# The opening of a hybrid RG-LRU / attention block: norm chain split between two engines, transposes placed ahead of the scale columns, shift sums kept in the query rows' tile

## Chip, cores and metric

One core of one Trainium2 chip runs the whole block. The metric is the device time of one execution in microseconds. Engines are named as in the profile: PE (TensorE), with its weight loads as PEld, DVE (VectorE), ACT (ScalarE), POOL (GpSimd) and SP (SyncE, which issues most DMAs).

## The reference

One layer (DEPTH = 1) over a sequence of 2048 rows of width 1024, batch 1, all in fp32:

```python
mod = silu(c) @ w_ada + b_ada
shift, scale, gate = split(mod, 3)
h = layer_norm(x) * (1 + scale) + shift
xr, zr, q, k, v, za, fl = split(h @ w_in)            # 512 columns each, fl: 8
xc = causal_depthwise_conv(xr, conv_w, conv_b)       # 4 taps
y_r = rms_norm(rg_lru(xc)) * silu(zr)
y_a = rms_norm(forgetting_attention(q, k, v, log_sigmoid(fl + b_fgate))) * silu(za)
y = concat([y_r, y_a]) @ w_out
out = layer_norm(2 ** 0.25 * x + gate * y) * ln_gain + ln_bias
```

What matters here is the beginning: `shift` and `scale` are products of one row, silu(c), with 1024 x 1024 parts of `w_ada`; `h` needs them both and the normalised x; the first projection is xr, from the first 512 columns of `w_in`.

## The kernel before

The sequence is cut into four chunks (ci = 0 to 3) of 512 rows, each chunk into four tiles of 128 rows, and the width of 1024 into eight slices k of 128. The work is written as one long Python program. Buffers are tiles of named tags with a fixed number of slots (t2: 10 slots of 2 KB a partition, r4: 8 of 4 KB, xr: 5, H: 8; PSUM banks: A 3, O 1, B 2, C 2). A tile waits until the one that had its slot before is done. A planner lays out each engine's order from simulated times, the earlier line of the program first among what is ready. `tc.issue_after(ins)` forces what follows to stand behind `ins` in the queue of the engine that `ins` is on. On the chip each engine then takes its queue strictly in that order. `tick()` moves the first of the small waiting chains (generators in `chains`) by one `yield`; `flush()` drains them.

The opening, up to about 145 us, goes through these stages:

1. **Warm-up and norm of chunk 0.** `spin(n)` issues n matmuls on zeros. `load_x(0)` loads four tiles as two halves each; `norm_x` calls `norm_tile` (L270) for each: `ln_stats` (L241) takes the statistics on DVE (L244, L246), adds epsilon (`ve`, L248), POOL raises to the power -0.5 (`rs`, L250), and DVE multiplies minus the mean by that (`nm`, L252). Then ACT (L274) or POOL (L276) applies scale and bias to each half.
2. **Chunk 0 in fp32 (loop at L759).** For each k: `scale_col(k)` (L638) loads a 128-column block of `w_ada` as `wadab`, sums part of it on DVE (L646, L648) for k of 2 and more, and does the rest as narrow matmuls `psc`; the result is one column of `Acol`, 1 + scale (L653). `load_w32(k)` loads a slice of `w_in` and splits it into a high and a low part (ACT L661, POOL L663). `make_h32(0, k, xs)` (L380) transposes four tiles on PE (`ptr`, L387), and ACT (L388) and DVE (L389) write h times scale as a high and a low part; POOL joins them for later (L378). `xr32` (L610) does twelve matmuls `pj` of slice k - 1. `col_max` (L167, tile `xam`) takes the largest magnitude of the weights, whose scale `xmax_fin` (L793) finishes with two small PE steps `pam`. From k = 5 on, the tiles of chunk 1 are normalised. At k = 7 the slabs 0 to 4 of the shift are begun by `shift_slab` (L746): each loads two tiles `wsh` in t2; ACT multiplies by the column of silu(c) (L231), POOL adds (L234) into `pa`, which is the tile of slab 0.
3. **Chunk 1 in fp32 (loop at L801).** Again `make_h32` and `xr32`, two k behind. The slabs 5 to 7 of the shift go to DVE: slab 5 is multiplied in place (L225) and becomes `va`, the others are added to it (L227). At k = 3 chunk 2 is loaded into t2, eight halves, and `va` and `pa` are added (L812). At k = 4 sixteen narrow matmuls `pada` make the shift column `Bcol`, and `make_scale` (L337) is put in `chains`; it finds the common scale `sh` through `all_max` (L148), with PE steps `pam`, and scales `Ash`, `Bcol` and `B16`. At k = 3 to 6 the weights are split to fp16 (`split_T`, L316, L317), and at k = 4 to 7 chunk 2 is normalised.
4. **Chunks 2 and 3 in fp16 (loops at L852 and L868).** `make_hk` (L394) transposes (L398), ACT writes h (`hf`, L400), ACT and DVE split it to fp16 (`hT`, L354, L355); `xr_k` projects slice k - 1; `finish_h` turns the kept h of chunks 0 and 1 into the same form.

After this come v, the gates, k, z, q and attention, which the diff does not touch. `QB`, four tiles of 67 rows for the query side of attention, is allocated at L905; the first use of its other rows is a memset on POOL (L1302), of which the planner puts the first four at the very beginning (2.9 us).

Of the kernel before, what the change touches and what calls it, by code (L numbers as in the profile page):

```python
# [10 lines left out]
F16 = mybir.dt.float16  # L11
F32 = mybir.dt.float32
# [26 lines left out]
def hybrid_mixer(  # L39
# [200 lines left out]

    def ln_stats(halves, eps):  # L241
        st = sm([P, 2, 6], "bst")
        for g in range(2):
            nc.vector.bn_stats(st[:, g, :], halves[g])  # L244
        mv = sm([P, 2], "mv")
        nc.vector.bn_aggr(mv, st)  # L246
        ve = sm([P, 1], "ve")
        last["ve"] = nc.vector.tensor_scalar(ve, mv[:, 1:2], eps, None, ALU.add).ins  # L248
        rs = sm([P, 1], "rs")
        last["pow"] = nc.gpsimd.tensor_tensor(out=rs, in0=ve, in1=mhalf[:, 0:1], op=ALU.pow).ins  # L250
        nm = sm([P, 1], "nm")
        nc.vector.scalar_tensor_tensor(nm, mv[:, 0:1], -1.0, rs, ALU.mult, ALU.mult)  # L252
        return rs, nm
# [15 lines left out]

    def norm_tile(hv, n):  # L270
        rs, nm = ln_stats(hv, EPS)
        for g in range(2):
            if g < n:
                nc.scalar.activation(hv[g], hv[g], AF.Identity, scale=rs, bias=nm)  # L274
            else:
                last["pow"] = nc.gpsimd.tensor_scalar(hv[g], hv[g], rs, nm, ALU.mult, ALU.add).ins  # L276
# [60 lines left out]
    def make_scale():  # L337
# [5 lines left out]
        nc.vector.scalar_tensor_tensor(bd, ma, 32.0, mb, ALU.mult, ALU.add)  # L343
        yield
        bda = yield from all_max(bd, 1, 1)
# [33 lines left out]

    def make_h32(ci, k, xs):  # L380
        if k % 2 == 0:
            h32[ci, k // 2] = sb.tile([P, 2, 2, CH], F32R, name="h32", tag="H", bufs=8)
        t = h32[ci, k // 2]
        ps = bank("C", "ptr")
        ks = slice((k % 4) * P, (k % 4 + 1) * P)
        for i in range(4):
            nc.tensor.transpose(ps[:, i * P:(i + 1) * P], xs[i][k // 4][:, ks], ident)  # L387
        hi_act[ci, k] = nc.scalar.activation(t[:, k % 2, 0], ps, AF.Copy, scale=Acol[:, k:k + 1]).ins  # L388
        last["lo"] = nc.vector.scalar_tensor_tensor(t[:, k % 2, 1], ps, Acol[:, k:k + 1], t[:, k % 2, 0],  # L389
                                                    ALU.mult, ALU.subtract).ins  # L390
        if ci == 0:
            join(0, k, h0f(k))
# [353 lines left out]
    def shift_slab(k, after):  # L746
        for g in range(2):
            w = t2([P, CH], "wsh")
            nc.sync.dma_start(w, w_ada_v[k, :, g * CH:(g + 1) * CH])
            if k < 5:  # L750
                with tc.issue_after(after):
                    pa[g] = ada_add_pool(pa[g], w, k)
            else:
                va[g] = ada_add(va[g], w, k)

    xam = cst([P, 4, KT], "xam")
    pss = [bank(t, "pj") for t in "AAAO"]
    spin(22)
    for k in range(KT + 1):  # L759
        if k < KT:  # L760
            with tc.issue_after(last["x0"]), tc.issue_after(last["pe"]):
                scale_col(k)
                load_w32(k)
            with tc.issue_after(last["pe"]):
                make_h32(0, k, xs)
            if k < 2:
                spin(4)
        if k == 4:
# [6 lines left out]
        if 5 <= k < 5 + 4:  # L775
            norm_tile(xs1[k - 5], 1)
        if k == KT - 1:
            for n in range(5):
                shift_slab(n, hi_act[0, n + KT - 5])
        if k > 0:  # L780
            with tc.issue_after(last["pe"]):
                xr32(pss, 0, k - 1)
            with tc.issue_after(last["lo"]):
                col_max(w32[k - 1][:, 0].rearrange("p (j n) -> p j n", n=P), AX.X, xam[:, :, k - 1])
    xr32_out(pss, 0)
    pss = [bank(t, "pj") for t in "BBAA"]
    pss = [bank(t, "pj") for t in "BBAA"]
# [4 lines left out]

    def xmax_fin():  # L793
        xcol = sm([P, 4], "xcol")
        nc.vector.tensor_reduce(out=xcol, in_=xam, axis=AX.X, op=ALU.max)
# [5 lines left out]
    for k in range(KT + 2):  # L801
# [6 lines left out]
        if k == 3:  # L808
            xs2 = load_x(2)
            with tc.issue_after(last["lo"]):  # L810
                for g in range(2):
                    nc.vector.tensor_tensor(va[g], va[g], pa[g], ALU.add)  # L812
        if k > 1:
            xr32(pss, 1, k - 2)
        tick()
        if 3 <= k < 3 + 4:
            with tc.issue_after(last["lo"]), tc.issue_after(hi_act[1, k]):
                wu.append((split_T(xraw[k - 3], xrec[:, k - 3:k - 2]), xun[:, k - 3:k - 2]))
        if k == 4:
# [8 lines left out]
            chains.append(make_scale())  # L828
            tick()
        if 4 <= k < 8:  # L830
# [18 lines left out]
    pss = [bank(t, "pj") for t in "AOBB"]  # L849
    new_h(2)  # L850
    new_h(0)
    for k in range(KT + 1):  # L852
        if k < KT:
            make_hk(2, k, xs2)
        if k > 0:
            xr_k(2, k - 1)
        if k < KT:
            with tc.issue_after(hi_act[2, k]),tc.issue_after(last["pow2"]):
                finish_h(0, k)
        if k == 4:  # L860
# [43 lines left out]
    nc.scalar.dma_start(kb[:, 0:1, :].rearrange("h a s -> a h s"), crow[0:1].unsqueeze(1).broadcast_to([1, H, S]))  # L904
    QB = [cst([67, CH], f"qb{i}", F16) for i in range(4)]  # L905
    Z = [cst([P, 4, 68], f"Z{i}", F16) for i in range(4)]
# [768 lines left out]
```

## Time and profile before

| | us |
|---|---|
| median of 3 runs | 1149.67 (1149.29 to 1150.42) |
| the profiled execution | 1150.82 |
| its span, first to last instruction | 1149.1 |
| PE busy | 1091.7 (95%) |
| DVE busy | 787.0 (68%) |
| ACT busy | 707.1 (62%) |
| POOL busy | 627.7 (55%) |
| mean granted TensorE clock | 0.977 of full speed |

The profile's engine rows give busy time; a busy share is a mean over stages with different limits. In the timeline, each row is a run of like instructions: start, length, engine, line, operation, output <- input, shape, count, and in brackets the idle time of the engine ahead of it with what ended it. In the windows, each row is a stretch, with its length, busy time (and instructions) of each engine asked for, the granted clock, the mean share of the 16 DMA engines and GB/s. Times count from the span's start.

### The profile page before, as it was taken

The page shows a single profiled execution, that of the slowest core. Times are in us where ns is not written, and L with a number is a line of the kernel's source. Part 1 is how long each engine was busy: PE and PEld are TensorE (multiplying, and loading weights), DVE is VectorE, ACT ScalarE, POOL GpSimd, SP SyncE. Part 2 cuts the span into 40 slices and gives each one's busy share as a digit, 9 for nine tenths or more (in the row PEclk, how much of TensorE's full clock was granted, in tenths as well). Part 3 has the DMA queues.
Part 4 walks back from the last instruction along what each step waited for, and adds up shares of the span by engine and source line. Part 5 has one row for each costly group of instructions (what it writes and reads, how often), then busy time and mean ns, then how long its engine had stood idle before and what let it go on. Part 6 is the DMA issues. An engine that isn't in the chain of part 4 may idle for free.

```text
span 1149.1 us, 20239 instructions
## 1 busy us (share of the span) xinstructions
PE 1091.7 (95%) x7473; PEld 611.2 (53%) x7473; DVE 787.0 (68%) x1441; ACT 707.1 (62%) x1234; POOL 627.7 (55%) x655
## 2 busy tenths in 40 slices
PE   8989999999999999999989999999999989999897
PEld 5875544454544444444455545556555555655544
DVE  6878577776777973585287556777777777787546
ACT  3447737664767511543286668787778877787930
POOL 5725633454455300730279756777777676766731
PEclk8999999999999999999979999999999999999999
DMA  9853047220224711764154354333233142321011
GB/s 285 242 172 110 1 127 217 77 68 19 55 56 119 229 66 52 251 203 142 36 187 145 108 161 136 97 96 100 91 106 114 35 137 82 103 74 47 19 47 55
DMA packets 109415, 128.36 MB, mean 112 GB/s; under 512 B 10316, under 2 KB 79540, under 8 KB 109316
## 3 DMA queue, kind: packets, MB, share of 16 engines
q1 hardware_dynamic: 109088, 127.01, 36.2%
q8 instruction: 58, 0.95, 0.3%
q14 instruction: 41, 0.34, 0.1%
q10 hardware_dynamic: 228, 0.06, 0.0%
HBM read 97.57 MB, written 29.46 MB: 111 GB/s over the span
## 4 chain that ended last, share of the span: by engine, by line
PE 65%; DVE 11%; ACT 8%; issue 6%; POOL 5%; DMA 4%; SPq 0%; DVEq 0%; ACTq 0%; POOLq 0%
PE pj L93 25%; PE pout L93 12%; PE pst L93 8%; PE pq L93 6%; PE acc L93 5%; PE pmx L93 4%; DVE mc L1315 2%; POOL ph L1347 1%; PE pgate L93 1%; ACT pf L1343 1%; DVE xres L1442 1%; DMA zs<-zd 1%; POOL XL L636 1%; ACT ph L1345 1%; DVE wadab L648 1%
## 5 line engine op out<-in xcount | busy, mean ns | idle before, releaser
L93 PE MATMUL pj<-hT,wT 128*128 128x512 f16 x1440 | 321.1, 381 | 2.6 <-DVE sza L1192 2.6
L1347 POOL TENSOR_TENSOR ph<-pf,ph 128x512 f16<-128x512 f32 (+2 forms) x240 | 263.8, 1111 | 108.5 <-ACT ph L1345 92.6
L93 PEld LDWEIGHTS <-wT 128*128 128x128 f16 x1792 | 169.8, 98 | 205.3 <-issue 18.8
L1315 DVE TENSOR_REDUCE mc<-pmx 128x1 f32<-128x512 f32 (+2 forms) x320 | 183.3, 601 | 90.2 <-PE pmx L93 84.1
L1343 ACT ACTIVATE pf<-pst,bias 128x512 f32<-128x512 f32 (+1 forms) x320 | 194.3, 632 | 59.4 <-PE pst L93 57.7
L1345 ACT CAST ph<-pf 128x512 f16<-128x512 f32 (+1 forms) x320 | 173.3, 568 | 21.4 <-PE acc L93 15.4
L93 PE MATMUL acc<-V,ph 128*128 128x129 f16 (+1 forms) x2176 | 159.6, 209 | 9.0 <-POOL ph L1347 4.4
L93 PEld LDWEIGHTS <-ph 128*128 128x128 f16 x2176 | 126.5, 99 | 67.8 <-POOL ph L1347 8.8
L93 PE MATMUL pst<-qs,kk 128*128 128x512 f16 (+1 forms) x320 | 111.6, 351 | 4.1 <-DVE mc L1315 2.9
L93 PE MATMUL pst<-qb,kk 65*128 65x512 f16 (+1 forms) x320 | 110.5, 354 | 0.9 <-ACT qb L1330 0.8
L93 PE MATMUL pmx<-kk,qb 67*128 67x512 f16 (+2 forms) x320 | 104.1, 353 | 4.5 <-DVE mc L1315 2.7
L93 PE MATMUL pout<-wo,yT 128*128 128x512 f16 (+1 forms) x396 | 97.2, 372 | 1.5 <-ACT yT L1423 1.5
L93 PE MATMUL pout<-wo,yr 128*128 128x512 f16 (+1 forms) x396 | 91.5, 373 | 1.5 <-DVE zs L1422 1.5
L93 PE MATMUL pj<-wN,hT 128*128 128x512 f16 x384 | 89.4, 378 | 0.2 <-ACT XL L847 0.2
L1243 POOL TENSOR_TENSOR XL<-XL,szr 128x512 f32<-128x512 f32 x16 | 22.8, 1428 | 111.7 <-ACT szr L1240 111.7
L93 PE MATMUL pq<-hT,wT 128*128 128x512 f16 x288 | 69.0, 393 | 3.1 <-DVE qhl L917 3.0
L1349 DVE TENSOR_TENSOR ph<-pf,ph 128x512 f16<-128x512 f32 (+1 forms) x80 | 54.8, 685 | 24.0 <-ACT ph L1345 23.2
L93 PEld LDWEIGHTS <-hT 128*128 128x128 f16 x640 | 44.6, 96 | 48.5 <-issue 3.3
L93 PEld LDWEIGHTS <-kk 65*128 65x128 f16 (+1 forms) x640 | 53.8, 99 | 29.2 <-issue 8.2
L93 PEld LDWEIGHTS <-yr 128*128 128x128 f16 x396 | 37.6, 98 | 39.3 <-issue 2.2
L93 PEld LDWEIGHTS <-yT 128*128 128x128 f16 x396 | 37.3, 97 | 38.6 <-ACT yT L1423 1.7
L491 POOL TENSOR_TENSOR xl<-xc,xh 128x512 fp32r<-128x512 f32 x16 | 23.1, 1446 | 57.0 <-ACT xh L489 55.6
(311 smaller groups left out, 1796.1 us busy)
## 6 DMA issues: line engine op xcount, KB each, us to landing
wraw<-in_w_in_dram SPq DMA_DIRECT2D x40, 512.0 KB
woraw<-in_w_out_dram SPq DMA_DIRECT2D x16, 512.0 KB
xres<-in_x_dram SPq DMA_DIRECT2D x16, 512.0 KB
out_dram<-xres SPq DMA_DIRECT2D x15, 512.0 KB
xt<-in_x_dram SPq DMA_DIRECT2D x16, 256.0 KB
wadab<-in_w_ada_dram SPq DMA_DIRECT2D x8, 512.0 KB
xt<-in_x_dram SPq DMA_DIRECT2D x8, 512.0 KB
wsh<-in_w_ada_dram SPq DMA_DIRECT2D x16, 256.0 KB
```

The costliest lines, as they stand in the source:

```text
L93: m = nc.tensor.matmul(o, lhsT=l, rhs=r, start=st, stop=sp, skip_group_check=chk)
L491: nc.gpsimd.tensor_tensor(out=xl, in0=xc, in1=xh, op=ALU.subtract)
L636: nc.gpsimd.tensor_scalar(XL[j][:, sl], XL[j][:, sl], 1.0, cs[j], ALU.mult, ALU.add)
L648: nc.vector.scalar_tensor_tensor(sub, blk[:, q - 1], cact[:, q - 1:q], sub, ALU.mult, ALU.add)
L1243: nc.gpsimd.tensor_tensor(out=XL[j][:, sl], in0=XL[j][:, sl], in1=sz, op=ALU.mult)
L1315: nc.vector.tensor_reduce(out=mc[:, i, b:b + 1], in_=ps[:, 0:w], axis=AX.X, op=ALU.max)
L1343: nc.scalar.activation(pf32[:, 0:w], ps[:, 0:w], AF.Exp, scale=DH ** -0.5, bias=bias[:, ci, h, kt:kt + 1])
L1345: nc.scalar.copy(ph[:, 0, 0:w], pf32[:, 0:w])
L1347: nc.gpsimd.tensor_tensor(out=ph[:, 1, 0:w], in0=pf32[:, 0:w], in1=ph[:, 0, 0:w], op=ALU.subtract)
L1349: nc.vector.tensor_tensor(ph[:, 1, 0:w], pf32[:, 0:w], ph[:, 0, 0:w], ALU.subtract)
L1442: nc.vector.scalar_tensor_tensor(xt[:, ns], xt[:, ns], rs, late["lnb"][:, ns], ALU.mult, ALU.add)
```

## The change

- `ln_stats` gets a flag `pool`. With it, DVE only negates the mean (`ng`) and POOL multiplies by `rs`, right behind the power. Chunks 0, 2 and 3 use it; chunk 1 (False) does not.
- `make_h32` is cut into `tr_h32` (the four transposes, now recorded as the last PE work) and `out_h32` (the writes). In the loop of chunk 0, tr(k) comes ahead of scale_col(k). At k = 1, one spin and the projection of slice 0 come ahead of scale_col(1). Spins: 22 + 2 x 4 become 32 + 1. The column maximum of the weights comes one k later.
- The shift's accumulator `pa` becomes a tile of its own, `qa0` and `qa1`, written by ACT from slab 0; the four `QB` share these two tiles afterwards. Slab 5 is multiplied by ACT instead of DVE.
- In the loop of chunk 1, the block that makes `Bcol` comes ahead of `xr32`, and for k = 8 and 9 the chains are flushed and `make_hk(2, 0)` and `make_hk(2, 1)` come ahead of the last two `xr32`. The loop of chunk 2 runs two k ahead accordingly.
- `xmax_fin` begins with a `yield`; `make_scale` loses one, and a `tick()` goes. A repeated allocation of four PSUM banks goes.

```diff
-    def ln_stats(halves, eps):
+    def ln_stats(halves, eps, pool):
...
-        nc.vector.scalar_tensor_tensor(nm, mv[:, 0:1], -1.0, rs, ALU.mult, ALU.mult)
+        if pool:
+            ng = sm([P, 1], "ng")
+            nc.vector.tensor_scalar(ng, mv[:, 0:1], -1.0, None, ALU.mult)
+            last["pow"] = nc.gpsimd.tensor_tensor(out=nm, in0=ng, in1=rs, op=ALU.mult).ins
+        else:
+            nc.vector.scalar_tensor_tensor(nm, mv[:, 0:1], -1.0, rs, ALU.mult, ALU.mult)
...
         nc.vector.scalar_tensor_tensor(bd, ma, 32.0, mb, ALU.mult, ALU.add)
-        yield
         bda = yield from all_max(bd, 1, 1)
...
     def make_h32(ci, k, xs):
+        out_h32(ci, k, tr_h32(ci, k, xs))
+
+    def tr_h32(ci, k, xs):
+        ps = bank("C", "ptr")
+        ks = slice((k % 4) * P, (k % 4 + 1) * P)
+        for i in range(4):
+            last["pe"] = nc.tensor.transpose(ps[:, i * P:(i + 1) * P], xs[i][k // 4][:, ks], ident).ins
+        return ps
...
             if k < 5:
                 with tc.issue_after(after):
-                    pa[g] = ada_add_pool(pa[g], w, k)
+                    if k == 0:
+                        pa[g] = con.tile([P, CH], F32, name=f"pa{g}", tag=f"qa{g}")
+                        nc.scalar.activation(pa[g], w, AF.Copy, scale=cact[:, 0:1])
+                    else:
+                        ada_add_pool(pa[g], w, k)
+            elif k == 5:
+                with tc.issue_after(after):
+                    nc.scalar.activation(w, w, AF.Copy, scale=cact[:, k:k + 1])
+                va[g] = w
...
-    spin(22)
+    spin(32)
...
     for k in range(KT + 1):
         if k < KT:
+            with tc.issue_after(last["pe"]):
+                ps = tr_h32(0, k, xs)
+            if k == 1:
+                spin(1)
+                x32_mm(0)
             with tc.issue_after(last["x0"]), tc.issue_after(last["pe"]):
                 scale_col(k)
                 load_w32(k)
-            with tc.issue_after(last["pe"]):
-                make_h32(0, k, xs)
-            if k < 2:
-                spin(4)
+            out_h32(0, k, ps)
...
-            norm_tile(xs1[k - 5], 1)
+            norm_tile(xs1[k - 5], 1, False)
...
-        if k > 0:
-            with tc.issue_after(last["pe"]):
-                xr32(pss, 0, k - 1)
+        if k > 1:
+            x32_mm(k - 1)
             with tc.issue_after(last["lo"]):
-                col_max(w32[k - 1][:, 0].rearrange("p (j n) -> p j n", n=P), AX.X, xam[:, :, k - 1])
+                w_max(k - 2)
+    w_max(KT - 1)
     xr32_out(pss, 0)
     pss = [bank(t, "pj") for t in "BBAA"]
-    pss = [bank(t, "pj") for t in "BBAA"]
...
-        if k > 1:
-            xr32(pss, 1, k - 2)
-        tick()
-        if 3 <= k < 3 + 4:
...
             chains.append(make_scale())
-            tick()
+        if k >= KT:
+            if k == KT:
+                flush()
+                new_h(2)
+                new_h(0)
+            make_hk(2, k - KT, xs2)
+        if k > 1:
+            xr32(pss, 1, k - 2)
+        tick()
+        if 3 <= k < 3 + 4:
...
-    for k in range(KT + 1):
-        if k < KT:
-            make_hk(2, k, xs2)
-        if k > 0:
-            xr_k(2, k - 1)
-        if k < KT:
-            with tc.issue_after(hi_act[2, k]),tc.issue_after(last["pow2"]):
-                finish_h(0, k)
+    for k in range(KT):
+        if k + 2 < KT:
+            make_hk(2, k + 2, xs2)
+        xr_k(2, k)
+        with tc.issue_after(hi_act[2, k]), tc.issue_after(last["pow2"]):
+            finish_h(0, k)
...
-    QB = [cst([67, CH], f"qb{i}", F16) for i in range(4)]
+    qa = [con.tile([67, 2, CH], F16, name=f"qa{g}", tag=f"qa{g}") for g in range(2)]
+    QB = [qa[i // 2][:, i % 2, :] for i in range(4)]
```

## What was predicted

> **What bounds the kernel now.** I read the page's busy table first, then each engine's timeline in the stretch that the diff touches, then the windows with the granted clock.
>
> ```profile
> PE 1091.7 (95%) x7473; PEld 611.2 (53%) x7473; DVE 787.0 (68%) x1441; ACT 707.1 (62%) x1234; POOL 627.7 (55%) x655
> ```
>
> TensorE (PE) is busy 95% of the 1149.1 us span, so 57.4 us are left in which it idles. A gain comes from an idle gap closed, a half-clock stretch shortened, or warm-up work left out. The diff touches only the opening, the first 145 us or so. Three places stand out there. **The front**, in PE's timeline (start, length, operation; the bracket is the idle time before it and what ended it):
>
> ```profile
> 8.54 2.33 PE L93 MATMUL pw<-warm 128*128 128x512 f16 x10
> 13.45 2.20 PE L93 MATMUL psc<-cact,wadab 128*128 128x1 f32 x16 [2.58 <-DMA wadab<-in_w_ada_dram]
> ...
> 17.89 3.41 PE L93 MATMUL psc<-cact,wadab 128*128 128x1 f32 x16
> ...
> 23.62 3.83 PE L93 MATMUL pj<-h,w 128*128 128x512 f32 x12
> 27.29 0.95 PE L93 MATMUL psc<-cact,wadab 128*128 128x1 f32 x8
> ```
>
> The first useful projection (pj) starts at 23.62; before it PE does warm-up (pw) and scale columns (psc). From there to 58.88, where the second chunk's projections begin, PE pauses only once, for under 1 us. The clock is back at full at about 25.2. In the row below the third column is the granted clock; if only 0.5 and 1 occur, 0.71 over 2 us is 0.84 us at full.
>
> ```profile
> 24.00:26.00 2.00, 2.00 (x8) 0.71 1.06 396
> ```
>
> **Gap two** is 3.13 us of idle PE ahead of 63.20, with a half clock behind it until about 66.1, 2.9 us, half of which is lost: 1.5 us. Together 4.6 us.
>
> ```profile
> 58.88 1.18 PE L93 MATMUL pj<-h,w 128*128 128x512 f32 x4
> 63.20 0.37 PE L152 MATMUL pam<-ident,xcol 128*4 128x128 f32 x1 [3.13 <-DVE h L389]
> ```
> ```profile
> 62.00:64.00 2.00, 0.80 (x3) 0.68 0.01 5
> 64.00:66.00 2.00, 2.00 (x6) 0.50 0.36 108
> 66.00:68.00 2.00, 2.00 (x10) 0.97 0.80 252
> ```
>
> **Gap three** is 1.24 + 0.75 + 0.76 = 2.75 us between the last projections of chunk 1 and the first of chunk 2, with a half clock from 96.84 to about 100.25, 1.7 us lost. Together 4.45 us.
>
> ```profile
> 88.39 3.02 PE L93 MATMUL pj<-h,w 128*128 128x512 f32 x12
> 91.25 0.60 PE L398 MATMUL ptr<-ident,xt 128*128 128x128 f32 x4
> 93.08 0.44 PE L398 MATMUL ptr<-ident,xt 128*128 128x128 f32 x2 [1.24 <-ACT xt L274]
> 94.27 0.44 PE L398 MATMUL ptr<-ident,xt 128*128 128x128 f32 x2 [0.75 <-ACT xt L274]
> 95.47 1.32 PE L398 MATMUL ptr<-ident,xt 128*128 128x128 f32 x8 [0.76 <-ACT hf L400]
> 96.64 4.44 PE L93 MATMUL pj<-hT,wT 128*128 128x512 f16 x12
> ```
> ```profile
> 96.00:98.00 2.00, 1.99 (x10) 0.71 0.27 102
> 98.00:100.00 2.00, 2.00 (x6) 0.50 0.01 4
> 100.00:102.00 2.00, 2.00 (x13) 0.93 0.00 0
> ```
>
> **The change, part by part.**
>
> *Norm chain split.* In the first norm chain VectorE (DVE) waits for GpSimd's (POOL's) power before each tile's nm, and only then begins the next tile. The first and the third of these waits (the second is 0.67), then POOL's power for tile 3, then ScalarE's (ACT's) first weight cast and its norm of tile 3:
>
> ```profile
> 7.62 0.16 DVE L252 SCALAR_TENSOR_TENSOR nm<-mv,rs 128x1 f32<-128x1 f32 x1 [0.75 <-POOL rs L250]
> ...
> 12.53 0.16 DVE L252 SCALAR_TENSOR_TENSOR nm<-mv,rs 128x1 f32<-128x1 f32 x1 [0.56 <-POOL rs L250]
> ```
> ```profile
> 14.39 0.55 POOL L250 TENSOR_TENSOR rs<-ve,mhalf 128x1 f32<-128x1 f32 x1 [1.90 <-DVE ve L248]
> ```
> ```profile
> 14.07 0.62 ACT L661 CAST w<-wrow 128x512 fp32r<-128x512 f32 x1 [1.86 <-DMA wrow<-in_w_in_dram]
> ...
> 16.98 0.81 ACT L274 ACTIVATE xt<-xt,nm,rs 128x512 f32<-128x512 f32 x1
> ```
>
> With nm on POOL, DVE loses the three waits ahead of tile 3 (0.75 + 0.67 + 0.56 = 1.98 us); the new ng costs what the old nm did. Tile 3's power starts at 14.39 - 2.0 = 12.4 and takes 0.55. The 128x1 multiply on POOL isn't in this trace: it costs between nothing and the power's 0.55 on the same shape; I take 0.5, nearest to that row. So nm is ready at about 13.5 and ACT could finish tile 3 at 14.3. But a weight cast stands in ACT's queue that waits for its DMA until 14.07. If that stays ahead, tile 3 is done at about 15.4; if ACT's order stays as it is, at 17.8 as now (16.98 + 0.81). I take **15.5** for the end of the first four transposes.
>
> *Transposes ahead of scale columns.* The new PE order is: spins, tr(0), psc(0), tr(1), one spin, projection 0, psc(1), tr(2), psc(2), projection 1. Now tile 3's transpose stands behind all of psc(1), 17.89 to 21.3. The 32 spins end at about 8.54 + 20 x 0.233 = 13.2 (ten took 2.33), ahead of tr(0), so they cost nothing. psc(0) takes 2.20 by its row, 3.41 by psc(1)'s at half clock; I take 2.6. Acol, hand-offs and the 0.7 us in which ACT writes h add 1.1. The first projection begins at 15.5 + 2.6 + 1.1 = **19.2**, 4.4 us earlier; with tile 3 between 14.3 and 17.8, at 18.2 to 21.6.
>
> Most of that is given back. psc(1), now hidden ahead of 23.62, comes behind projection 0: 16 matmuls at the rate of 8 in 0.95, 1.9 us. And PE does little dense work between 13.2 and 19.2, so projection 0 would start at half clock. Now only 25.2 - 23.62 = 1.6 us of the pj stretch are at half (0.8 lost). After gaps two and three it took 2.9 and 3.6 us of dense work until full clock; with bad luck two such stretches, 6 us. I take 4.8 us, 2.4 lost. The end of this stage, 58.9 now, becomes 19.2 + (58.9 - 23.6) - 0.8 + 1.9 + 2.4 = 58.0: **-0.9 us**, bounds -3 and +2.
>
> *Shift sums.* Gap two hangs on one DVE instruction, here with the two behind it, and POOL's last add with what follows it:
>
> ```profile
> 58.31 4.16 DVE L225 TENSOR_SCALAR wsh<-wsh,cact 128x512 f32<-128x512 f32 x1 [0.52 <-DMA wsh<-in_w_ada_dram]
> 62.40 0.74 DVE L389 SCALAR_TENSOR_TENSOR h<-ptr,Acol,h 128x512 fp32r<-128x512 f32 x1
> 63.06 0.47 DVE L225 TENSOR_SCALAR wsh<-wsh,cact 128x512 f32<-128x512 f32 x1
> ```
> ```profile
> 60.91 1.28 POOL L234 TENSOR_TENSOR wsh<-wsh 128x512 f32<-128x512 f32 x1
> 82.23 0.55 POOL L250 TENSOR_TENSOR rs<-ve,mhalf 128x1 f32<-128x1 f32 x1 [20.03 <-DVE ve L248]
> ```
>
> The same operation takes 0.47 us once POOL is quiet and 4.16 us while POOL's adds run, to 62.19. Behind it stands the DVE half of h for which PE waits. The diff moves this slab (k = 5) to ACT: two more instructions of about 0.7 us each, on an engine that idles there:
>
> ```profile
> 69.40 0.69 ACT L388 ACTIVATE h<-ptr,Acol 128x512 fp32r<-128x512 f32 x1 [8.16 <-PE ptr L387]
> ```
>
> The accumulator pa moves into the query rows' tile, which frees two of the ten t2 buffers, so that the slab loads that wait on SyncE's queue for buffers (the row gives the sum, the count and the longest) start sooner:
>
> ```profile
> SPq L749 <- POOL wsh L234: 9.9, 5, 5.8
> ```
>
> What is late next? The DVE adds of slabs 6 and 7 have two SBUF inputs, as the wadab sums have, whose shortest, median and longest time differ like this:
>
> ```profile
> L648 DVE SCALAR_TENSOR_TENSOR wadab<-wadab,cact x18: 333/352/1296, 18.6 to 48.6; 128x128 f32<-128x128 f32 x18
> ```
>
> The longest is one POOL add longer than the median, so the slab adds may be blocked as well. The page SBUF — State Buffer of the Trainium skill, section Who interferes with whom, says so: a DVE instruction with two SBUF inputs and a GpSimd one that reads SBUF exclude each other for a whole instruction; the trace agrees (1.296 against 0.352 us). But they follow slab 5 on ACT, and so the first h, and 12 projections, 2.8 us, cover one block of 1.28. I leave 0.5 us and count **-4.1** of the 4.6. The query rows' memsets on POOL now wait for pa; POOL idles 20 us ahead of 82.23, so nothing is counted.
>
> *Chunk 2's first rows ahead.* make_hk(2,0) and (2,1) now stand ahead of the last 24 projections of chunk 1, which at 12 in 2.86 us (88.39 to 91.25) are 5.7 us of cover for the transposes, hf and hT that PE waits for in gap three. For this the scale sh must come sooner: one yield fewer in make_scale and the earlier place of pada give it about one k, some 3.2 us. And xs2's norms must come sooner: DVE loses its waits for the power here too, and the loads get the freed buffers. DVE is loaded in this stage (third of the busy columns, 8.57 of 10 us), so norms may still be a little late:
>
> ```profile
> 80.00:90.00 10.00, 10.00 (x50) 7.94 (x49) 8.57 (x25) 4.48 (x6) 2.90 (x5) 1.00 0.51 147
> ```
>
> I leave 1.0 us: **-3.4** of the 4.45.
>
> Sum: 1150.82 for the profiled run (span 1149.1 and 1.7 around it), less 0.9 + 4.1 + 3.4 = 8.4, is 1142.4. The profiled run lies 1.15 above the median, 1149.67; on that level the forecast is **1141.3 us**. PE is the busiest engine by far, so a shift of the opening should reach the end.
>
> **Rivals.**
>
> *One gap stays* (0.20). Either the adds of slabs 6 and 7 block the h in front of PE as L225 does now: 1149.67 - 0.9 - 3.4 = 1145.4; or xs2's norms are still late: 1149.67 - 0.9 - 4.1 = 1144.7. For it: POOL's blocks and DVE's load, shown above. Against it: the freed buffers.
>
> *The clock holds in the front* (0.10). If the time between the spins and the dense work doesn't drop the clock, psc(0) takes 1.9 and the 2.4 us are not lost: the front gives 0.9 + 0.7 + 2.4 = 4.0, the sum is 11.5, the time 1138.2. For it: only about 2 us of PE idle remain ahead of tr(0). Against it: 2.58 us idle followed by psc at 13.45 did drop it. The page TensorE: Matmul & The Clock Gate of the Trainium skill, section HAM oscillation — how this bites in real kernels, asks for no idle gap over about 3.4 us, so by it this gap would be harmless; the trace shows a half clock after idle gaps of 2.58 and 3.13 us.
>
> *It does not do what it says* (0.12). Both waits come back under other names, since the order on each engine is laid out anew by planned times: 1149.67 - 0.9 = 1148.8, no change.
>
> *PE parks at the moved transposes* (0.12). In PE's order chunk 2's transposes now stand ahead of 24 projections. Tile 3 of xs2 is normalised at 94.2 now. PE comes to them at 91.25 - 5.5 (front and gap two, the latter whole) - 5.7 = 80.0. If the norm stayed at 94.2, PE would wait 14 us, then do 0.7 of transposes and 5.7 of projections and lose 1.7 by the clock: 102.3, against 96.64 + 1.7 = 98.3 now. That is 4.0 us slower, 1153.7. It decides where tile 3 comes later than 90.2. Against it: that norm hangs on loads and DVE work that also come earlier.
>
> **How the numbers follow.** The forecast has 0.46. The time is its own, 1141.3, by its bounds 1138.5 to 1144.5. The range takes in the full clock and one gap left, 1136.5 to 1148.5, and leaves out the last two rivals. A difference of 0.2%, 2.3 us, is about what a measurement of this kernel can tell from no change. Faster: 0.46 + 0.20 + 0.10 = 0.76; same 0.12; slower 0.12.
>
> **What would show it.** Right: the first pj at 18 to 22; no DVE instruction of 4 us and no idle PE near 58 to 62, with the clock at 1.0; the first pj with hT, wT within 1.5 us of the last with h, w. Wrong: psc(1) still ahead of projection 0; DVE adds of 1.3 us and more ahead of an h on which PE waits; idle PE ahead of transposes, ended by ACT's xt; or an opening 8 us shorter and a later gap grown by as much.

## The result, and the profile after

The changed kernel takes 1157.07 us (median of 8 runs, 1152.88 to 1162.19) against 1149.58 (8 runs, 1148.47 to 1151.29) on the same chip: ratio 1.0064, 95% interval [1.0045, 1.0082]. It is 7.5 us slower; 1141.3 was forecast, and the time lies outside the range. The profiled execution took 1157.4 us, with a span of 1155.6.

The busy table of the changed kernel:

```profile
PE 1094.0 (95%) x7476; PEld 612.9 (53%) x7476; DVE 777.7 (67%) x1439; ACT 709.0 (61%) x1236; POOL 635.3 (55%) x667
```

PE's busy time grew by 2.3 us only; most of the 6.5 us by which the span grew is idle PE. Three stretches answer to those of the forecast, and a fourth, far behind the opening, had not been looked at.

**The front** of the changed kernel, in PE's timeline:

```profile
17.16 0.33 PE L391 MATMUL ptr<-ident,xt 128*128 128x128 f32 x1 [2.15 <-ACT xt L279]
17.32 2.46 PE L93 MATMUL psc<-cact,wadab 128*128 128x1 f32 x16
...
20.76 5.09 PE L93 MATMUL pj<-h,w 128*128 128x512 f32 x12
25.68 1.84 PE L93 MATMUL psc<-cact,wadab 128*128 128x1 f32 x16
...
28.76 0.57 PE L93 MATMUL psc<-ones,wadab 128*128 128x1 f32 x2
32.32 3.99 PE L93 MATMUL pj<-h,w 128*128 128x512 f32 x10 [3.00 <-ACT h L398]
```

Tile 3's transpose waits for its norm until 17.16, projection 0 starts at 20.76 at half clock (12 in 5.09), and a new wait of 3.00 us stands ahead of projection 1. Chunk 1 begins at 65.31 instead of 58.88. What that wait is made of stands in the queues of DVE and ACT (the next two fences, the same stretch):

```profile
26.08 1.28 DVE L244 BATCH_NORM_STATS2 bst<-xt 128x6 f32<-128x512 f32 x2
...
28.52 0.16 DVE L257 SCALAR_TENSOR_TENSOR nm<-mv,rs 128x1 f32<-128x1 f32 x1 [0.66 <-POOL rs L250]
28.60 1.28 DVE L244 BATCH_NORM_STATS2 bst<-xt 128x6 f32<-128x512 f32 x2
29.80 0.14 DVE L663 SCALAR_TENSOR_TENSOR Acol<-psc,c_ada 128x1 f32<-128x1 f32 x1
```
```profile
31.06 0.62 ACT L671 CAST w<-wrow 128x512 fp32r<-128x512 f32 x1 [1.53 <-DMA wrow<-in_w_in_dram]
31.59 1.26 ACT L398 ACTIVATE h<-ptr,Acol 128x512 fp32r<-128x512 f32 x2
```

The second scale column was summed on PE by 27.5 (25.68 + 1.84), but DVE took the norms of chunk 1, which its queue had first, and wrote `Acol` at 29.80; on ACT the h that needs it stood behind a weight cast that waited for its load until 31.06. PE was ready at 29.33 (28.76 + 0.57). With `Acol` ready at 29.94 and 0.7 us for ACT's h, I estimate that DVE's order accounts for about 1.3 us of the 3.00 and the cast for the rest.

**Gap two** is closed. The windows of the changed kernel, then of the one before:

```profile
60.00:80.00 20.00, 20.00 (x108) 1.00 0.51 171
```
```profile
60.00:80.00 20.00, 16.87 (x86) 0.91 0.55 169
```

**Gap three** is still there. PE's and ACT's timelines in the changed kernel:

```profile
92.42 1.17 PE L93 MATMUL pj<-h,w 128*128 128x512 f32 x4
...
95.74 0.44 PE L408 MATMUL ptr<-ident,xt 128*128 128x128 f32 x2 [1.94 <-ACT xt L279]
96.44 0.44 PE L408 MATMUL ptr<-ident,xt 128*128 128x128 f32 x2 [0.26 <-ACT xt L279]
97.64 1.97 PE L408 MATMUL ptr<-ident,xt 128*128 128x128 f32 x8 [0.76 <-ACT hf L410]
99.40 4.88 PE L93 MATMUL pj<-hT,wT 128*128 128x512 f16 x12
```
```profile
92.93 2.05 ACT L629 COPY XL<-pj 128x512 f32<-128x512 f32 x4 [1.77 <-PE pj L93]
94.84 1.54 ACT L279 ACTIVATE xt<-xt,nm,rs 128x512 f32<-128x512 f32 x2
```

2.96 us of waits against 2.75 before. PE waits for the norms of tiles 2 and 3 (the two `xt` at 94.84). DVE's, then POOL's timeline show when their inputs came:

```profile
90.43 0.75 DVE L399 SCALAR_TENSOR_TENSOR h<-ptr,Acol,h 128x512 fp32r<-128x512 f32 x1 [0.70 <-ACT h L398]
...
92.86 1.27 DVE L244 BATCH_NORM_STATS2 bst<-xt 128x6 f32<-128x512 f32 x2
```
```profile
93.59 0.19 POOL L255 TENSOR_TENSOR nm<-ng,rs 128x1 f32<-128x1 f32 x1
...
95.28 0.19 POOL L255 TENSOR_TENSOR nm<-ng,rs 128x1 f32<-128x1 f32 x1
```

Tile 2's nm is ready at 93.78, and four copies of chunk 1's result keep ACT from it until 94.84. Tile 3's nm is ready only at 95.47, just as ACT comes to it: its statistics (92.86) stand in DVE's queue behind those of tile 2 and behind DVE's half of the last h of chunk 1 (90.43). So the end of gap three is set by DVE's queue, and the copies delay tile 2 alone.

**Chunk 0's attention** is the fourth place. PE's waits from 560 to 720 us (sum, count, longest), the rows for POOL's and ACT's part, of the kernel before, then of the changed one:

```profile
PE acc L93 <- POOL ph L1347: 1.3, 1, 1.3
```
```profile
PE acc L93 <- POOL ph L1378: 4.7, 4, 1.6
PE acc L93 <- ACT ytmp L1396: 2.8, 2, 1.8
```

And one window inside it, before and after: PE loses 4.3 us and the clock falls to 0.83.

```profile
600.00:620.00 20.00, 19.65 (x156) 0.95 0.51 158
```
```profile
600.00:620.00 20.00, 15.40 (x98) 0.83 0.49 150
```

The diff doesn't touch a line there. But the programs differ: compared by operation and operand, the order of DVE, ACT and POOL behind the opening is the old one except in a stretch from some 590 to 665 us.

### The profile page after: what moved, and what is told of

It is laid out like the page before. It is cut to its first block, busy times and chain, and to the rows that moved or that the text cites. A ratio compares the mean times of both kernels' runs of the same rounds, so it can differ in the third digit from the quotient of the medians.

```text
span 1155.6 us, 20267 instructions
## 1 busy us (share of the span) xinstructions
PE 1094.0 (95%) x7476; PEld 612.9 (53%) x7476; DVE 777.7 (67%) x1439; ACT 709.0 (61%) x1236; POOL 635.3 (55%) x667
## 4 chain that ended last, share of the span: by engine, by line
PE 67%; DVE 10%; ACT 8%; DMA 5%; POOL 5%; issue 4%; SPq 1%; ACTq 0%; DVEq 0%; POOLq 0%
PE pj L93 29%; PE pout L93 13%; PE pst L93 7%; PE acc L93 5%; PE pmx L93 4%; PE pq L93 4%; DVE mc L1346 3%; POOL ph L1378 2%; PE pgate L93 1%; ACT pf L1374 1%; DVE xres L1473 1%; ACT ph L1376 1%; DMA wadab<-in_w_ada_dram 1%; ACT L525 1%; POOL woraw L1080 1%
## 5 line engine op out<-in xcount | busy, mean ns | idle before, releaser
L93 PE MATMUL pst<-qa,kk 65*128 65x512 f16 (+1 forms) x320 | 111.0, 356 | 0.9 <-ACT qa L1361 0.8
L93 PE MATMUL pmx<-kk,qa 67*128 67x512 f16 (+2 forms) x320 | 104.8, 354 | 4.4 <-DVE mc L1346 2.9
L93 PE MATMUL pj<-h,w 128*128 128x512 f32 x192 | 54.6, 435 | 3.1 <-ACT h L398 3.0
```

What stands on the lines that cost most here:

```text
L93: m = nc.tensor.matmul(o, lhsT=l, rhs=r, start=st, stop=sp, skip_group_check=chk)
```

## Experiments

Each ratio is against the kernel before, on the chip of its own job; there, the kernel before had medians of 1148.9, 1150.0, 1148.85 and 1148.69.

**The change in four parts.** Norm chain split alone:

```diff
-    def norm_tile(hv, n):
+    def norm_tile(hv, n, pool=True):
...
-            norm_tile(xs1[k - 5], 1)
+            norm_tile(xs1[k - 5], 1, False)
```

> Of the whole change only the norm split (POOL multiplies by the power for chunks 0, 2 and 3). Theory 1: DVE's statistics of chunk 0 end 2 us earlier, but ACT's cast that waits for a weight load stands ahead of tile 2, so the first projection comes within 1.5 us of 23.62; chunk 2's norms up to 2 us earlier; 1147 to 1150 us. Theory 2: drift of up to 4 us behind 560 us.

1148.52 us, ratio 0.9984 [0.9964, 1.0003], within the first expectation's range. The first projection came at 20.04, not within 1.5 us of 23.62; what that start is worth is told below.

The new loop of chunk 0 alone:

```diff
-    spin(22)
+    spin(32)
...
+            with tc.issue_after(last["pe"]):
+                ps = tr_h32(0, k, xs)
+            if k == 1:
+                spin(1)
+                x32_mm(0)
...
```

> Of the whole change only the new order of chunk 0's loop (transposes first, slice 0's projection ahead of scale column 1, 32 + 1 spins, column maxima one k later). Theory 1, the front's order is what costs: the first projection at 20 to 22 us, but a wait of PE of 2 us or more for h of slice 1, a half clock behind it, and chunk 1's projections beginning at 63 to 66 (58.9 before); gap two may remain, so 1154 to 1159 us. Theory 2, the opening costs little and the later stages drift with any new plan: chunk 1 begins within 2 us of 58.9, and the time moves by up to 4 us to either side, with the difference arising behind 560 us.

1156.46 us, ratio 1.0057 [1.0034, 1.0081]: nearly the whole loss. Chunk 1 starts at 63.03, as the first theory has it, though PE waits 1.36 us and not 2 or more for the h of slice 1; and later stages lost as well.

The shift's own accumulator, slab 5 on ACT, and the shared query tiles alone:

```diff
+                        pa[g] = con.tile([P, CH], F32, name=f"pa{g}", tag=f"qa{g}")
+                        nc.scalar.activation(pa[g], w, AF.Copy, scale=cact[:, 0:1])
...
+            elif k == 5:
...
```

> Of the whole change only the shift sums: pa in the query rows' tile, slab 5 on ACT. Theory 1: gap two (3.13 us idle and a half clock) is gone, nothing else moves, 1144 to 1147 us. Theory 2: gap two is gone, but the later stages drift, 1142 to 1153 us, with a difference behind 560 us that no wait of the opening explains.

1150.4 us, ratio 1.0009 [0.9992, 1.0026]. Of gap two, 1.68 us stayed, where both theories had it gone. DVE's timeline, then PE's, in this kernel:

```profile
56.81 6.33 DVE L227 SCALAR_TENSOR_TENSOR wsh<-wsh,cact 128x512 f32<-128x512 f32 x4 [1.23 <-ACT wsh L759]
```
```profile
63.65 0.38 PE L93 MATMUL pam<-amd,ones 4*128 4x4 f32 x2 [1.68 <-DVE ma L339]
```

The adds of slabs 6 and 7 are what is late next, much as one rival had it: four of them take 6.33 us, and POOL's adds run until 60.61. PE waits here for a small maximum (`ma`) behind them, not for h.

The loops of chunks 1 and 2 (the rows of chunk 2 ahead) alone:

```diff
...
+        if k >= KT:
+            if k == KT:
+                flush()
+                new_h(2)
+                new_h(0)
+            make_hk(2, k - KT, xs2)
         if k > 1:
             xr32(pss, 1, k - 2)
...
```

> Of the whole change only the second loop: the shift column and chunk 2's first two slices ahead of projections, the yields and the tick, the bank allocation. Theory 1: gap three shrinks little, since ACT's norms of chunk 2 come as late as before: first projection with hT, wT between 95 and 97.5 (96.64 before), 1147 to 1151 us. Theory 2: the same at 97 us, but the time drifts by up to 4 us behind 560 us.

1154.3 us, ratio 1.0041 [1.0026, 1.0057]. Yet its first v projection came at 147.55, against 149.81 and 148.74 in two profiles of the kernel before: an opening 1 to 2 us shorter, and an end 4.7 us later by the ratio, above what either theory allowed.

These two slow parts are also the two whose order in chunk 0's attention differs from before; norm_alone and shift_alone keep it. Hence the next four.

**The order in chunk 0's attention, with nothing changed but the number of warm-up matmuls.** One or two matmuls on zeros move the simulated times by which the order is laid out. First, the changed kernel with one less, which gives it the old order behind the opening:

```diff
-    spin(32)
+    spin(31)
```

> The changed kernel with 31 warm-up matmuls in place of 32. Its opening is ordered as in the changed kernel, but the planner lays out everything behind about 150 us, the attention of chunk 0 among it, as in the kernel before (the changed kernel's own order there differs between 570 and 665 us). Theory 1, the opening costs all of it: 1154 to 1158 us as the change. Theory 2, the other order in chunk 0's attention costs 4 to 5 us: 1149 to 1152 us. If both have a part, 1151 to 1155.

1150.97 us, ratio 1.0012 [0.9999, 1.0025]: six of the 7.5 us are gone. Then the kernel before with two more, which gives it another order there:

```diff
-    spin(22)
+    spin(24)
```

> The kernel before with 24 warm-up matmuls in place of 22, ahead of a wait of PE that is longer than they take. Its opening keeps the order of before, but the planner lays out chunk 0's attention nearly as in the changed kernel. Theory 1: as the kernel before within 1.5 us. Theory 2: 4 to 5 us slower, 1152 to 1155 us, with more PE waits for ytmp and ph between 570 and 665 us.

1154.74 us, ratio 1.0039 [1.0025, 1.0053]. The opening's code is that of before, and the loss is 4.7 us against its own job's 1150.0. The opening's order moved in places too, but it didn't lose: the first v projection comes at 146.02. Then home_alone with the old order:

```diff
-    spin(22)
+    spin(23)
```

> home_alone with 23 in place of 22 warm-up matmuls: the same edit of the second loop, with the order behind about 150 us that the kernel before has. Theory 1: 1153 to 1156 us as home_alone. Theory 2: 1147 to 1150 us, so that home_alone's 5 us were the order of the attention.

1149.69 us, ratio 0.9999 [0.9986, 1.0012]: home_alone's loss is gone. And the kernel before, profiled once more:

> The kernel before once more, for a second profile. If the front of the first profile was typical: first projection at 23 to 24 us and chunk 1's projections at 58 to 60. If it was a late start: first projection at 19.5 to 21.5 and chunk 1's at 56.5 to 58.5, as in shift_alone and norm_alone, whose order is the same there.

1149.82 us; its first projection starts at 19.02 and its chunk 1 at 57.99, so the first profile's start was the later one. PE's waits for POOL's `ph` from 560 to 720 us in before_24_spins and in after_31_spins:

```profile
PE acc L93 <- POOL ph L1347: 6.0, 5, 1.8
```
```profile
PE acc L93 <- POOL ph L1378: 1.7, 2, 1.3
```

PE's waits for POOL's `ph` go with the order, not with the opening: 1.3 to 2.1 us in before, before_again, home_23_spins and after_31_spins, 4.7 to 6.0 in the changed kernel, front_alone, home_alone and before_24_spins. POOL's and PE's timelines in before_24_spins show one of them, and POOL's in after_31_spins the same spot in the old order:

```profile
597.31 1.28 POOL L1347 TENSOR_TENSOR ph<-pf,ph 128x512 f16<-128x512 f32 x1
598.55 2.49 POOL L1049 TENSOR_TENSOR woraw<-woraw,gbc 128x512 f32<-128x512 f32 x2
601.00 2.44 POOL L1347 TENSOR_TENSOR ph<-pf,ph 128x384 f16<-128x384 f32 x2
```
```profile
602.41 0.78 PE L93 MATMUL acc<-V,ph 128*128 128x65 f16 x10 [1.85 <-POOL ph L1347]
```
```profile
598.81 2.55 POOL L1080 TENSOR_TENSOR woraw<-woraw,gbc 128x512 f32<-128x512 f32 x2
601.32 4.00 POOL L1378 TENSOR_TENSOR ph<-pf,ph 128x512 f16<-128x512 f32 x3
```

In the other order two multiplies of the output weights (2.49 us, nobody waits for them yet) stand between two `ph` for which PE waits; in the old order the three `ph` come together.

The times of three pairs of kernels show that such a change of order costs 4.5 to 6 us. Where it is lost is shown for two pairs. From the first to the last q projection, a stretch that takes in chunk 0's attention, it is 139.2 and 138.6 us in the two profiles of the kernel before and 143.3 in before_24_spins, 139.8 in after_31_spins and 144.1 in the changed kernel. In home_alone it is 139.9, and 140.7 in home_23_spins, so the profiles don't place that loss. The other order isn't one order either: the four kernels that have one differ from each other, and in home_alone none of these multiplies stands between the `ph` of the longest wait, 3.30 us, and the `ph` before it. In the pair of the changed kernel the spin moved the opening too: in the profiles 1.9 us lie ahead of the first q projection (561.87 against 559.93). That the multiplies are the cause is read from the traces and was not tried by itself.

**What the opening gains without the new front.** Norm chain and shift sums together, in the old order:

> Only the norm chain split and the shift sums (own accumulator tile, slab 5 on ACT); the front loop, the loop of chunk 1 and the query rows' own four tiles are as before. The order of the engines behind the opening is that of the kernel before. If the opening's gains reach the end (theory 1: the new front alone eats them), chunk 1 starts at about 57.5 and takes 30 instead of 32.4 us, and the time is 1146 to 1148, ratio 0.996 to 0.999. If only the order of the later stages counts (theory 2 by itself), it is 1149.5 to 1150.5, ratio 1.000.

1149.29 us, ratio 0.9992 [0.9977, 1.0008], which lies between the two expectations and doesn't tell them apart. Chunk 1 starts at 57.99 and takes 29.5 us, as the first expected. Then the whole change without the new loop of chunk 0:

```diff
-    spin(22)
+    spin(26)
```

> The whole change without the new loop of chunk 0 (transposes stay behind the scale columns), with 26 warm-up matmuls so that the order behind the opening stays that of the kernel before. Theory 1: chunk 1 starts at 57 to 58.5, gap two is closed (chunk 1 takes 28.3 us as in the changed kernel), gap three is as there (5.7 us); the first v projection comes at 144 to 146 and the time is 1145 to 1148, ratio 0.996 to 0.998. Theory 2 by itself: 1149 to 1151, ratio 1.000.

1146.72 us, ratio 0.9978 [0.9961, 0.9995]. Chunk 1 starts at 57.07 and the first v projection comes at 144.45, as expected of the first theory; chunk 1 takes 29.4 us and not 28.3, since 0.94 us of gap two stay. In a second job:

> The same kernel as no_new_front, once more, beside the next one. If its gain is real, the ratio is 0.996 to 0.9995 again; if it was the spread between executions, it is 0.9995 to 1.002.

1148.07 us, ratio 0.9991 [0.9974, 1.0007]. The two together make a gain of 1 to 2 us likely; only one interval leaves out no change. With the norms of chunk 2 one k earlier:

```diff
-        if 4 <= k < 8:
-            norm_tile(xs2[k - 4], 1)
+        if 3 <= k < 7:
+            norm_tile(xs2[k - 3], 1)
```

> no_new_front with the norms of chunk 2 one k earlier. In scale_first_early_norms the same edit cut the way from the last projection of chunk 1 to the first of chunk 2 from 5.8 to 4.9 us in the profiles. If that passes to the end: 0.5 to 1.5 us below no_new_front_again; if it is used up in the later stages: the same within 0.5 us.

1146.74 us, ratio 0.9987 [0.997, 1.0004], 1.3 us below no_new_front_again by the medians, which the intervals can't tell apart. None of these beats the kernel before by more than a quarter of a per cent.

**Why the new front loses.** First, the scale column of slice 1 back ahead of projection 0:

```diff
+            with tc.issue_after(last["x0"]), tc.issue_after(last["pe"]):
+                scale_col(k)
+                load_w32(k)
             if k == 1:
                 spin(1)
                 x32_mm(0)
-            with tc.issue_after(last["x0"]), tc.issue_after(last["pe"]):
-                scale_col(k)
-                load_w32(k)
```

> The whole change with its 32 warm-up matmuls, but at k = 1 the scale column stands ahead of the spin and of the projection of slice 0, as before. The order behind the opening is that of the kernel before. If the projection of slice 0 ahead of scale column 1 is what makes PE wait 2.7 to 3.0 us for the second h (theory 1), that wait falls below 1 us, chunk 1 starts at 58 to 60 instead of 62.3 to 65.3, and the time is 1145.5 to 1148, ratio 0.996 to 0.998. If the wait comes from the late load of w_in slices or from DVE's statistics of chunk 1, whatever the place of projection 0, it stays above 2 us, chunk 1 starts at 62 or later and the time is 1150 to 1152.

1153.82 us, ratio 1.0038 [1.0019, 1.0057]: the first theory fell. The 3.00 us wait is gone, as that theory has it, and chunk 1 still starts at 65.18, because another came. PE, then POOL, then DVE of this kernel:

```profile
45.44 0.79 PE L391 MATMUL ptr<-ident,xt 128*128 128x128 f32 x4 [2.40 <-DVE h L399]
46.03 1.71 PE L93 MATMUL psc<-cact,wadab 128*128 128x1 f32 x8
```
```profile
31.42 1.27 POOL L673 TENSOR_TENSOR w<-wrow,w 128x512 fp32r<-128x512 f32 x1 [2.45 <-ACT w L671]
32.64 0.56 POOL L250 TENSOR_TENSOR rs<-ve,mhalf 128x1 f32<-128x1 f32 x1
```
```profile
33.23 0.16 DVE L257 SCALAR_TENSOR_TENSOR nm<-mv,rs 128x1 f32<-128x1 f32 x1 [3.45 <-POOL rs L250]
```

DVE stands 3.45 us at the norm of chunk 1's second tile, whose power on POOL is queued behind a weight split that waits for ACT's cast and so for a load. What DVE has put off comes out late at 45. With the norms of chunk 2 earlier too:

> As scale_column_first, and the norms of chunk 2 one k earlier (k = 3 to 6 instead of 4 to 7), so that on ACT three of the four tiles are normalised ahead of the four copies of chunk 1's result instead of two. If gap three stays because these norms are late, the wait for xt of 1.94 us goes down by 0.8 to 1.9 us, from the last projection of chunk 1 to the first of chunk 2 it takes 4 to 5 us instead of 5.7, and the time is 0.5 to 2.5 us below scale_column_first (1144 to 1147). If the statistics delay the DVE half of h in chunk 1 by as much, it is the same as scale_column_first within 0.5.

1153.0 us, ratio 1.0029 [1.0014, 1.0044], 0.8 us below scale_column_first, which the intervals can't tell apart. From the last projection of chunk 1 to the first of chunk 2 it takes 4.9 us instead of 5.8, but the longest wait is as it was, now for one tile (PE, then ACT):

```profile
94.41 0.44 PE L408 MATMUL ptr<-ident,xt 128*128 128x128 f32 x2 [1.93 <-ACT xt L279]
```
```profile
91.60 2.05 ACT L629 COPY XL<-pj 128x512 f32<-128x512 f32 x4 [1.99 <-PE pj L93]
93.52 0.84 ACT L279 ACTIVATE xt<-xt,nm,rs 128x512 f32<-128x512 f32 x1
```

With tile 3's nm ready earlier (on POOL at 92.04 + 0.19), ACT's four copies hold it up by 1.3 us. So once DVE's statistics come sooner, the copies are what holds gap three open next.

Then chunk 1's norms held back on DVE, in the changed kernel:

```diff
...
-            norm_tile(xs1[k - 5], 1, False)
+            with tc.issue_after(lo0[min(k - 5 + 2, KT - 1)]):
+                norm_tile(xs1[k - 5], 1, False)
```

> The changed kernel (32 warm-up matmuls, its new loop of chunk 0) with one thing held back: the norm of chunk 1's tile i stands on DVE behind the low half of h of slice i + 2. The order behind the opening is that of the kernel before. Theory F1 (chunk 1's norms, laid ahead of Acol and h on DVE and waiting there for POOL's power, cost the front 4 to 6 us): PE's wait for the second h falls below 1 us, no DVE wait for POOL rs ahead of an Acol, chunk 1 starts at 57 to 60, the time is 1145.5 to 1148, ratio 0.996 to 0.999. Theory F2 (the front itself costs: transposes ahead of the scale column, half clock, loads of w_in that land late): chunk 1 still starts at 61 or later, time 1150 to 1153.

1151.81 us, ratio 1.0035 [1.0019, 1.0051]. Half right: the wait for the second h is gone, as F1 has it, but chunk 1 starts at 63.48, as F2 has it. PE's timeline:

```profile
28.60 3.02 PE L93 MATMUL pj<-h,w 128*128 128x512 f32 x12
...
43.70 0.80 PE L391 MATMUL ptr<-ident,xt 128*128 128x128 f32 x4 [1.95 <-DVE c_vec L145]
...
46.28 5.13 PE L93 MATMUL pj<-h,w 128*128 128x512 f32 x12
```

Projection 1 begins at 28.60 without a pause (32.32 in the changed kernel). With the norms held back, ACT's h stands ahead of the weight cast as well (27.46 against 29.87), so the run takes away both parts of the wait at once. Behind it, 0.92 us are lost at 38.32, 1.95 at 43.70, and a projection at half clock takes 5.13 instead of 3.02. Both edits together:

> As scale_column_first, with the same hold on chunk 1's norms as late_norms. F1: the 2.4 us wait for the DVE half of h near 45 goes, chunk 1 starts at 57 to 60 instead of 65.2, the time falls by 4 to 6 us to 1146 to 1149. F2: it stays at 1151 to 1154.

1151.62 us, ratio 1.0026 [1.001, 1.0042]. In its profile chunk 1 starts at 59.93, as F1 expects, but the time did not fall to 1146 to 1149. The profile shows that the gain is not lost in the opening. At the last q projection (696.06) this kernel is 3.2 and 2.2 us ahead of the two profiles of the kernel before (699.23 and 698.28), and at a wait near 920 (920.44 against 924.33 and 923.54) 3.9 and 3.1 us. Behind 940 it is 1.2 and 0.4 us ahead, by the same POOL instructions. In between, the order is the same and so are PE's three waits (0.20, 1.28 and 1.36 us; the first is 0.21 in the kernel before), but a longer half clock stands behind them. In the kernel before, then here:

```profile
920.00:940.00 20.00, 16.87 (x143) 0.91 0.52 158
```
```profile
920.00:940.00 20.00, 17.16 (x109) 0.74 0.57 172
```

By the clock, 0.74 against 0.91 over 20 us, 3.4 us more of full-speed work is lost here. Other kernels with the old order show either value in the profile (0.91 in before_again and after_31_spins, 0.74 in shift_alone, norm_and_shift and home_23_spins); what decides it is not shown.

All with a profile and a ratio, side by side (us from the span's start; "old" is the order of the kernel before in chunk 0's attention, "other" any other):

| kernel | new front | order | chunk 1 starts | ratio |
|---|---|---|---|---|
| the changed kernel | yes | other | 65.31 | 1.0064 |
| front_alone | yes | other | 63.03 | 1.0057 |
| scale_column_first | yes | old | 65.18 | 1.0038 |
| late_norms | yes | old | 63.48 | 1.0035 |
| scale_first_early_norms | yes | old | 63.78 | 1.0029 |
| scale_first_late_norms | yes | old | 59.93 | 1.0026 |
| after_31_spins | yes | old | 62.27 | 1.0012 |
| home_alone | no | other | 58.51 | 1.0041 |
| before_24_spins | no | other | 59.27 | 1.0039 |
| shift_alone | no | old | 57.02 | 1.0009 |
| home_23_spins | no | old | 57.92 | 0.9999 |
| norm_and_shift | no | old | 57.99 | 0.9992 |
| no_new_front_again | no | old | 58.36 | 0.9991 |
| no_new_front_early_norms | no | old | 55.61 | 0.9987 |
| norm_alone | no | old | 57.33 | 0.9984 |
| no_new_front | no | old | 57.07 | 0.9978 |

Two columns sort the ratios, and the start of chunk 1 does not: the five with the new front and the old order have a mean of 1.0028, the two with the other order alone 1.0040, and the seven with neither 0.9991. The first two excesses add up to 0.68%, or 7.8 us; the changed kernel, which has both, lost 7.5. That sum is rough: the five are different fronts, and the one among them with the change's own front, after_31_spins, has 1.0012, and its interval (0.9999 to 1.0025) doesn't leave out no change.

## Why the prediction was wrong, point by point

- **"A shift of the opening should reach the end."** This step failed: the gain was to pass through everything behind the opening. It took the rest of the kernel as fixed, but the order there is laid out by simulated times, and the change moved them. Another order in chunk 0's attention costs 4.5 to 6 us; by the ratios, it is 0.39% in before_24_spins, 0.42% between home_alone and home_23_spins, and 0.52% between the changed kernel and after_31_spins (4.5, 4.8 and 6.0 us of 1150). So of the 15.9 us between the forecast's -8.4 and the measured +7.5 about 6 belong to this step; the other 9.8 belong to the terms of the opening, which were to give 8.4 and cost 1.4. The rival "It does not do what it says" named the means, an order laid out anew by planned times; it looked for it in the opening only, and gave it no loss (1148.8).
- **The front, -0.9 with bounds -3 and +2.** Wrong in sign: chunk 1 starts 6.4 us later (65.31 against 58.88) in the profiled pair, and 1.1 to 6.4 us later than 58.88 in every kernel with the new front. Three things were off.
  - The first projection was to start 4.4 earlier than 23.62. That start was itself one of the late ones. In the second profile of the same kernel, before_again, PE's timeline has

```profile
19.02 2.11 PE L93 MATMUL pj<-h,w 128*128 128x512 f32 x8 [0.55 <-ACT h L388]
```

  so an execution can start as early without the change; 20.76 came out, where 19.2 was forecast. Over all profiles the first projection starts at 20.8 to 25.3 with the new front and at 19.0 to 24.0 without it.
  - Tile 3 was put at 15.5 with 17.8 as the bad bound. The bad bound held (17.16 + 0.33), since ACT's casts stayed ahead of tiles 2 and 3, as the forecast had allowed. POOL's 128x1 multiply, put at 0.5, took 0.19.
  - What stood behind the moved work on DVE was not gone through: chunk 1's norms come ahead of Acol and h there and wait for POOL. late_norms shows that this order, with the weight cast that it puts ahead of h on ACT, made the wait of 3.00 us. Taking it away moved the loss to slices 3 and 4 and did not end it.
- **Gap two, -4.1.** Right in its place and size: no idle PE from 60 to 80, and chunk 1 takes 28.3 us (65.31 to 93.59, the end of the row at 92.42) against 32.5 before, 4.2 less. But the forecast gave it to the shift sums alone, and it takes all parts together: shift_alone left 1.68 us behind the adds that the rival *One gap stays* named, and the change without the new front left 0.94.
- **Gap three, -3.4.** Wrong: 2.96 us of waits against 2.75. The step that failed is "xs2's norms must come sooner": tile 3's came 2.8 us behind the last projection of chunk 1 (96.38 against 93.59), as before (94.2 against 91.41). DVE lost its waits for the power, but its queue has the statistics of tiles 2 and 3 behind the last h of chunk 1, so they move along with chunk 1's end. The rival *One gap stays* had named DVE's load and these norms; the copies on ACT, next in line, had not been looked at for this stage.
- **The rival "PE parks at the moved transposes"** did not come about. Tile 3 was normalised at 96.4 (94.84 + 1.54), far behind the 90.2 from which it was to decide, but the transposes of tiles 2 and 3 were laid behind the last projections again, so PE worked on.
- In sum, the opening with the old order behind it (after_31_spins) gave +1.4 us, 0.12% of 1150, by the interval not clear of nothing, where -8.4 was forecast.

What stays open: why the kernels with a repaired front still lose 3 us. With both edits the profiled opening is nearly clean up to gap three, and yet the twelve runs are 0.26% slower than the kernel before. Their profile puts the loss at the half clock near 925 us, but one profile may not be typical of them: its execution took 1150.06 us, 1.6 below the median, and single executions of the kernel before spread from 1143.4 to 1153.2 in the same job. Neither tile 3's statistics ahead of the last h nor ACT's copies behind the last norm was tried in the changed kernel's own front.

## What to carry to other kernels

Where a planner lays out the order, compare the whole order before and after a change, not the edited lines: one or two matmuls on zeros at the start changed the order of stages 500 us later, and the time by 0.4 to 0.5%, more than any gain of this opening. Before an instruction is moved ahead, read on every engine what the queue has between it and its consumer, in-order waits for loads included. Take the start of a stage from two executions before building a saving on it. And follow a gain from stage to stage to the end: in scale_first_late_norms 2 to 3 us of it reached 696 us, and most was gone at 940.

## What the runs showed of the hardware

- Two executions of the same kernel (before and before_again) start the first projection at 23.62 and at 19.02 us, and their spans differ by 1.0 us only.
- Half clock followed idle gaps well below 3 us. In scale_column_first 8 `psc` took 1.71 us after 2.40 us of idle PE, against 0.95 in the row for the same work at full clock (27.29 in the kernel before). In late_norms a half clock followed 1.95 us, and near 925 us it followed waits of 0.20, 1.28 and 1.36 us in a row. In no_new_front a gap of 0.94 us did not drop it; PE's timeline:

```profile
63.28 0.27 PE L152 MATMUL pam<-ident,xcol 128*4 128x128 f32 x1 [0.94 <-DVE h L393]
63.31 2.55 PE L93 MATMUL pj<-h,w 128*128 128x512 f32 x10
```

  The Trainium skill, page TensorE: Matmul & The Clock Gate, section HAM oscillation — how this bites in real kernels, asks for no idle gap above about 3.4 us. By that rule neither the 2.40 nor the 1.95 us would have mattered; here the measurement differs. What part the narrow matmuls and transposes around these gaps have in it was not separated.
- Four DVE adds with two inputs in SBUF took 6.33 us when they began beside POOL's adds (shift_alone, L227, 1.64 each by the mean), against a mean of 0.74 for the same four in the kernel before, which run from 63.46 on, behind POOL's last add (over at 62.19). This agrees with what the Trainium skill, page SBUF — State Buffer, section Who interferes with whom, says of the two engines excluding each other.
